# A conditioned decoder trunk on one core: another list of the order of issue

## The chip, the cores and the metric

One core of a Trainium2 chip runs the kernel. The metric is device time in microseconds (us) of one execution, as a median of several. The engines of the core work side by side, each through its own row of instructions in order: TensorE (PE, with its weight loads as PEld), VectorE (DVE), ScalarE (ACT), GpSimd (POOL) and SyncE (SP), which here issues the transfers (DMA) of the weights. An instruction that waits holds up all that stand behind it on its engine. So the same instructions in another order can take another time.

## The reference

Two layers of a decoder trunk on one sequence of 256 tokens of 1024 features (fp32). Each layer normalises x, scales and shifts it by vectors that are made from the conditioning vector c (adaLN: c times `w_ada`), projects it, runs attention, multiplies by a SiLU gate path, projects back, multiplies by the adaLN gate and adds the result to x. A last RMS norm ends it.

```python
def masked_softmax(s, mask, sink=None):
    s = jnp.where(mask, s, -jnp.inf)
    m = jnp.max(s, axis=-1, keepdims=True)
    ...
    return e / jnp.where(den > 0, den, 1.0)

# layer 0: heads "A": sliding window 128 with sinks (8 heads, 1 key head)
#          heads "B": compressed + selected + window branches, gated (8 heads, 2 key heads)
# layer 1: 16 heads, blocks of 256 keys, which with 256 tokens is plain causal attention
```

The weights that have to be read make up most of the 70.29 MB that the profile shows as read.

## The kernel before

**How products are made.** All products of weights are in a split form: a weight tile of 1 MB is loaded into one of five buffers `raw_101` to `raw_105`, ACT casts it to a high half (`whi`), and DVE subtracts that from the original for a low half (`wlo`). The activations have such halves too (`hhi`, `hlo` of the normalised x; `ghi`, `glo` of the attention's output). Three matmuls (`mm3`) then stand for each product: high by high, high by low, low by high. They add up in the PSUM banks `ps_pj`.

**The opening.** The weights `w_in_even` and the adaLN weights come in pieces, and the first projections run on them row block by row block (`start_ada`, `start_row`, `start_sums`, `start_prep`, `start_mm`). The adaLN vector of a block is added up on DVE (`acc`) or PE, transposed into `ps_m`, and made into scale and shift (`shs`). DVE and ACT then use `shs` to make the block's `oT`, `hhi` and `hlo`.

**adaLN later.** For the second layer and for the gates `ada_wide` loads four tiles of `w_ada` to a vector into the same five buffers. DVE multiplies and adds two rows of each to the accumulator (`acc<-raw,cz,acc`, 1024 wide), and the buffer is free after the second of them.

**Attention.** Scores land in `ps_s` (or in `ps_pj`, `ps_m`). DVE masks them and takes the minimum (`late,mn<-ps_s,tb`, printed as ISA or CUSTOM_DVE with a tiny row `mn` behind it), ACT takes the exponential, DVE scales by `rc`, and PE transposes three pieces into the one bank `ps_pt`, from where ACT copies them. `pcT` holds the same for narrower heads, `oT` receives the heads' output, `t` the outputs of projections before they are transposed.

**Parts of the array.** `ada_shift_scale`, `start_sums`, `attn_four`, `attn_values`, `attn_quad` and `compress` use matmuls that fill a part of the array (`tile_position`); those of one set are handed to `plan.group`, which gives each of them all that the set depends on.

**What sets the order.** Nothing is issued as the code is walked. Each call is recorded by `Plan.record` with the calls that it depends on, and `issue` then goes through a list of their numbers, `ORDER`. The engines' rows follow from that list. Since all instructions are issued there, all have that one line in the profile, L249.

```python
    def issue(self):
        place = {i: n for n, i in enumerate(ORDER)}
        assert len(place) == len(ORDER) == len(self.ops)
        for i in ORDER:
            assert all(place[d] < place[i] for d in self.ops[i]["deps"])
            self.ops[i]["inst"] = self.ops[i]["fn"]()
```

Buffers are chosen when a call is recorded, so they do not change with the list.

Of the kernel before, what the change touches and what calls it, by code (L numbers as in the profile page):

```python
# [37 lines left out]
0 2 1 4 5 44 9 685 3 10 6 37 88 11 7 38 35 12 87 13 89 14 15 16 86 17 18 85 19 70 90 20 91 21 71 22 92 55 72 23 93 47  # L38
45 24 41 56 25 48 74 57 26 49 94 73 27 28 40 59 58 80 95 42 29 75 50 30 76 104 60 61 62 51 63 77 78 98 65 64 66 67 106
107 108 109 110 111 112 113 114 115 116 52 117 101 79 118 119 120 121 122 123 124 125 126 127 128 129 53 105 130 131  # L40
132 133 134 135 136 137 96 68 97 138 81 145 139 82 31 69 140 83 32 141 100 33 142 147 34 146 99 182 170 149 164 148
183 151 171 143 150 173 84 179 167 102 165 144 158 185 152 186 176 153 103 177 159 178 156 172 154 174 212 200 201 157
213 160 180 184 155 168 162 206 222 36 187 224 194 166 531 175 225 169 195 181 215 188 226 203 189 207 223 202 227 214
228 229 230 231 232 233 234 235 236 161 237 238 239 240 241 242 243 220 244 245 163 246 247 190 248 197 191 198 208
249 204 217 192 257 196 250 209 251 216 259 252 205 199 258 210 274 261 211 253 286 260 283 255 275 295 254 289 530
268 287 262 193 256 277 219 276 290 218 264 296 292 272 288 221 270 284 273 280 269 281 322 266 293 285 334 263 294
324 282 271 278 291 323 297 335 279 307 313 319 267 325 308 314 310 332 301 265 302 336 316 326 304 303 333 337 338
339 340 341 342 343 344 345 346 347 348 349 329 350 351 352 353 354 355 356 357 305 358 320 309 306 311 327 365 312
359 298 367 317 366 328 299 315 330 360 318 361 321 368 362 300 433 363 371 384 369 436 390 402 364 385 393 370 403
405 529 378 391 437 399 396 373 386 331 372 397 374 394 435 380 379 398 420 387 382 438 432 400 376 401 406 404 381  # L50
423 434 388 407 439 389 421 534 408 392 383 411 440 528 395 429 409 687 414 375 424 441 425 430 377 442 443 444 445
446 447 448 449 450 451 452 453 417 454 415 426 455 418 412 413 456 463 422 457 532 459 410 458 416 533 431 464 427
465 682 480 467 419 466 461 492 489 501 460 478 495 481 469 483 468 486 470 476 484 479 502 683 462 482 474 485 428
490 684 471 491 496 475 507 472 497 513 8 504 477 503 505 506 473 493 498 540 499 541 514 932 555 508 509 686 525 557
487 556 519 809 515 537 526 527 558 538 488 500 543 535 494 510 539 607 520 551 516 511 608 542 553 559 517 552 521
536 518 512 554 545 522 549 560 550 546 565 609 566 544 561 934 562 563 617 564 610 571 931 567 572 568 569 690 616
936 573 629 619 620 621 933 611 622 523 570 630 623 577 612 578 574 575 576 618 524 579 583 580 613 581 688 584 585
586 582 638 589 590 631 624 614 632 637 633 625 591 592 626 634 671 627 587 593 689 588 628 595 596 597 598 635 599
600 640 547 641 636 639 642 643 594 548 601 602 644 603 658 604 605 606 659 650 645 646 664 647 651 648 665 652 653
649 654 660 692 655 691 693 694 661 657 662 695 696 656 697 698 663 699 700 666 810 701 702 935 703 670 704 667 668  # L60
705 672 706 707 669 708 938 709 1014 812 710 811 673 674 956 937 742 39 743 43 744 46 745 675 746 813 747 748 749 940
941 942 943 944 945 946 947 957 1021 756 959 960 961 962 963 964 965 966 939 1024 750 948 949 950 951 754 952 953 954
955 751 676 755 958 677 757 967 968 969 970 971 972 973 974 752 1131 678 753 1209 776 679 975 711 54 774 680 1212 712
778 713 714 758 780 715 782 976 759 977 775 978 760 761 979 681 762 716 768 980 864 865 866 779 867 981 868 615 982
874 869 870 781 871 983 872 777 990 984 985 878 986 987 717 783 896 718 880 719 989 764 763 784 720 902 721 722 723
875 988 724 876 725 991 785 1022 769 992 726 787 727 728 993 729 898 765 766 730 900 731 732 786 767 733 734 994 735
1023 1025 736 995 737 738 739 770 771 772 901 996 792 1330 1026 773 1079 1080 1081 740 1082 1083 1084 903 1085 1086
741 873 788 1091 789 793 790 997 814 815 816 791 817 818 1089 897 998 999 1000 1001 1132 1027 819 820 821 822 823 824
1002 825 1109 826 879 827 1133 1003 794 828 829 877 830 831 832 881 1004 795 796 882 833 1111 834 835 836 1005 837 838
839 1115 840 841 842 1093 843 1116 844 845 1087 846 883 847 899 1113 848 849 1006 850 851 885 852 1210 853 854 855 797  # L70
856 857 858 904 859 1090 860 861 1028 1134 905 1135 862 1136 1137 1138 891 1139 1140 906 1141 884 1215 1337 1007 863
798 799 1338 800 907 801 1211 802 909 803 804 1110 805 886 1114 887 888 890 1029 1030 1088 1008 1031 1032 1033 1142
889 1034 914 1035 1036 1331 915 1037 1038 892 893 1143 894 1039 1040 1041 895 1042 1043 908 1044 1009 1045 1332 1046
1047 1112 1048 1049 910 911 1094 1050 1051 1052 1053 1146 1054 1092 1055 1415 1117 912 1010 1056 1057 1058 806 913
1059 1060 1061 1213 1062 1333 1011 1095 1164 1012 1063 1216 1064 916 917 918 1065 1066 1067 1013 919 1068 1096 1334
1069 1070 807 1071 1072 1073 1074 1015 1075 1165 1335 1148 1098 1214 1016 1149 1076 1017 1018 1104 1019 1166 920 921
1020 1414 922 1144 923 1077 924 1168 1411 925 1170 926 1147 927 1410 1118 1078 1267 1145 1268 1269 1270 1097 1120 1339
1099 1126 1100 1101 1217 1218 1150 1171 1219 928 1220 1221 1222 1102 1223 1224 1151 1340 1225 1226 1167 1227 1228 1229
1230 1169 1231 1232 1233 1153 1234 1103 1235 1236 1416 808 1237 929 1238 1239 1240 1407 1241 1172 1105 1275 1242 1436
1243 1125 1406 1244 1245 1152 1246 1279 1247 1248 1119 1249 1250 1173 1158 1434 1106 1107 1437 1251 1252 1253 1254  # L80
1255 1256 1257 1108 1258 1259 1260 1281 1438 1261 1262 1263 1435 1264 1121 1122 1123 1265 1271 1272 1273 1274 1124
1266 1494 1159 1127 1128 1297 1417 1129 1181 1442 1299 1443 1130 1444 1301 1445 1277 1440 1154 1303 1155 1156 1180
1341 930 1342 1157 1343 1344 1175 1174 1441 1160 1161 1278 1162 1446 1447 1163 1454 1455 1280 1439 1176 1177 1298 1178
1456 1457 1179 1458 1459 1351 1276 1182 1504 1355 1183 1300 1184 1408 1345 1185 1346 1347 1348 1302 1186 1304 1187
1371 1188 1375 1189 1282 1353 1190 1373 1191 1192 1193 1349 1374 1194 1305 1283 1195 1306 1196 1284 1197 1409 1356
1198 1199 1352 1200 1201 1202 1286 1203 1285 1204 1431 1307 1292 1205 1412 1287 1314 1430 1288 1289 1448 1449 1354
1450 1350 1451 1206 1452 1308 1453 1460 1357 1290 1291 1461 1358 1413 1534 1462 1293 1294 1295 1463 1464 1296 1465
1535 1491 1566 1207 1542 1309 1490 1310 1311 1466 1313 1543 1377 1312 1544 1545 1359 1360 1418 1315 1316 1317 1467
1546 1318 1472 1567 1372 1336 1361 1362 1366 1363 1419 1319 1376 1320 1321 1378 1322 1323 1536 1324 1325 1379 1326
1365 1505 1380 1327 1208 1328 1495 1364 1420 1421 1422 1423 1329 1382 1381 1367 1432 1368 1424 1369 1547 1473 1370  # L90
1468 1387 1474 1433 1388 1383 1384 1385 1475 1476 1386 1469 1568 1492 1425 1389 1390 1391 1569 1548 1392 1470 1537
1393 1394 1395 1396 1397 1493 1398 1399 1400 1401 1402 1426 1403 1570 1652 1471 1549 1404 1477 1506 1550 1405 1507
1484 1538 1485 1478 1720 1486 1487 1488 1539 1489 1479 1480 1481 1482 1428 1500 1483 1571 1572 1501 1540 1551 1552
1553 1496 1554 1502 1555 1541 1556 1557 1656 1558 1559 1654 1560 1561 1781 1562 1655 1563 1564 1565 1497 1573 1574
1590 1575 1498 1576 1577 1427 1591 1578 1499 1579 1580 1581 1592 1582 1583 1584 1657 1596 1585 1586 1429 1587 1588
# [1272 lines left out]
```

## Time and profile before

| | before |
|---|---|
| median of 3 runs | 298.81 us (298.41, 300.07, 298.81) |
| span of the profiled execution | 296.8 us |
| PE, DVE, ACT busy | 286.9, 252.2, 188.5 us |
| granted TensorE clock, mean | 0.992 |
| read from memory | 70.29 MB |

The page of the profile does not give the profiled execution's own time beside its span; the runs lie between 1.6 and 3.3 us above the span, and the median 2.0. The stages are found by the names in the trace: the opening to 45 us; the rest of layer 0 and its heads to about 155; the second layer's projections and heads to 252; its output projection to 290; and a tail of 6.4 us, in which the last rows are normalised and stored. A row of a timeline has start in us, duration in us, engine, line, operation, `out<-in`, shape and count, and in brackets the idle time ahead and what ended it.

### The profile page before, as it was taken

How to read it: one execution, taken by the hardware profiler on the slowest of the kernel's cores; microseconds unless marked ns; L12 is line 12 of the kernel's file. 1: busy time of each engine (PE TensorE's matmuls, PEld its weight loads, DVE VectorE, ACT ScalarE, POOL GpSimd, SP SyncE). 2: the span in 40 equal slices, each digit the busy share in tenths (PEclk: the TensorE clock that was granted, in tenths of full speed). 3: DMA queues.
4: the chain of work that ended last, by engine and by line, in shares of the span. 5: the costliest groups of instructions: out<-in, count | busy, mean ns of one | idle time of the engine just before them, and what ended most of it. 6: DMA issues, size and time to landing. Idle time of an engine off the chain costs nothing.

```text
span 296.8 us, 6205 instructions
## 1 busy us (share of the span) xinstructions
PE 286.9 (97%) x2297; PEld 246.3 (83%) x2297; DVE 252.2 (85%) x630; ACT 188.5 (63%) x479; POOL 9.2 (3%) x32
## 2 busy tenths in 40 slices
PE   8999999999999999999999999999999989999991
PEld 8778778897788978776768899998899989887891
DVE  0488698799999999999798679799959779999883
ACT  5356246876997899984638863286386338684531
POOL 2100000001000000000020000000000000000021
PEclk9999999999999999999999999999999999999996
DMA  7999999998992679686886969729828800192003
GB/s 242 389 389 377 344 394 372 300 355 240 390 386 71 235 252 352 210 281 212 305 264 190 367 179 301 275 79 311 300 93 280 280 9 2 42 380 75 3 0 141
DMA packets 48479, 71.73 MB, mean 242 GB/s; under 512 B 2522, under 2 KB 33986, under 8 KB 48450
## 3 DMA queue, kind: packets, MB, share of 16 engines
q1 hardware_dynamic: 47906, 70.92, 70.0%
q10 hardware_dynamic: 544, 0.43, 0.4%
q8 instruction: 18, 0.29, 0.4%
q14 instruction: 11, 0.09, 0.1%
HBM read 70.29 MB, written 1.05 MB: 240 GB/s over the span
## 4 chain that ended last, share of the span: by engine, by line
PE 77%; DMA 14%; DVE 4%; ACT 2%; issue 1%; SPq 1%; POOL 1%; DVEq 0%; ACTq 0%
PE ps_pj L249 53%; PE ps_pt L249 7%; PE ps_o L249 6%; PE ps_s L249 6%; PE ps_m L249 5%; DMA raw<-in_w_in_even_dram 5%; DMA qT<-in_w_ada_dram 4%; DMA raw<-in_w_ada_dram 3%; DMA late<-in_w_ada_dram 2%; DVE wlo L249 1%; ACT whi L249 1%; SPq L249 1%; DVE xs L249 1%; DVE t L249 1%; POOL parts L249 1%
## 5 line engine op out<-in xcount | busy, mean ns | idle before, releaser
L249 ACT CAST whi<-raw 128x512 fp32r<-128x512 f32 (+2 forms) x116 | 72.2, 656 | 23.6 <-PE ps_pj L249 18.5
L249 DVE TENSOR_TENSOR wlo<-raw,whi 128x512 fp32r<-128x512 f32 (+2 forms) x100 | 71.8, 741 | 8.9 <-ACT whi L249 8.8
L249 PE MATMUL ps_pj<-hlo,whi 128*128 128x256 f32 x256 | 69.8, 286 | 0.0
L249 PE MATMUL ps_pj<-hhi,wlo 128*128 128x256 f32 x256 | 69.6, 284 | 0.0
L249 PE MATMUL ps_pj<-hhi,whi 128*128 128x256 f32 x256 | 69.5, 286 | 0.0
L249 PEld LDWEIGHTS ps_pj<-hhi,wlo 128*128 128x128 f32 x256 | 47.4, 188 | 1.7 <-issue 1.3
L249 PEld LDWEIGHTS ps_pj<-hhi,whi 128*128 128x128 f32 x256 | 47.0, 188 | 1.1 <-issue 0.3
L249 PEld LDWEIGHTS ps_pj<-hlo,whi 128*128 128x128 f32 x256 | 47.1, 188 | 0.5 <-issue 0.2
L249 DVE SCALAR_TENSOR_TENSOR acc<-raw,cz,acc 128x1024 f32<-128x1024 f32 x24 | 30.7, 1278 | 2.1 <-DMA raw<-in_w_ada_dram 2.0
L249 ACT ACTIVATE late<-late,mn 128x128 f32<-128x128 f32 (+1 forms) x58 | 25.9, 448 | 8.4 <-DVE mn L249 8.4
L249 DVE SCALAR_TENSOR_TENSOR wlo<-raw,whi 128x512 fp32r<-128x512 f32 x32 | 21.4, 686 | 6.3 <-ACT whi L249 6.2
L249 PE MATMUL ps_pj<-whi,hhi 128*128 128x512 f32 (+2 forms) x72 | 25.7, 376 | 0.6 <-ACT hhi L249 0.5
L249 PE MATMUL ps_pj<-whi,hlo 128*128 128x512 f32 (+2 forms) x72 | 26.0, 372 | 0.0
L249 PE MATMUL ps_pj<-wlo,hhi 128*128 128x512 f32 (+2 forms) x72 | 25.6, 367 | 0.0
L249 ACT COPY late<-ps_pt 128x384 f32<-128x384 f32 (+1 forms) x29 | 14.0, 484 | 12.9 <-PE ps_pt L249 12.9
L249 PE MATMUL ps_pj<-whi,ghi 128*128 128x512 f32 (+1 forms) x56 | 20.8, 372 | 0.0
L249 PE MATMUL ps_pj<-wlo,ghi 128*128 128x512 f32 (+1 forms) x56 | 20.5, 366 | 0.0
L249 PE MATMUL ps_pj<-whi,glo 128*128 128x512 f32 (+1 forms) x56 | 20.4, 366 | 0.0
L249 PE MATMUL ps_pt<-ta,late 128*128 128x128 f32 x87 | 16.5, 278 | 0.9 <-DVE late L249 0.9
L249 PEld LDWEIGHTS ps_pj<-whi,hhi 128*128 128x128 f32 x72 | 13.5, 188 | 3.2 <-ACT hhi L249 1.2
L249 ACT ACTIVATE whi<-raw 128x512 fp32r<-128x512 f32 x16 | 10.0, 629 | 9.0 <-PE ps_pj L249 8.7
L249 PEld LDWEIGHTS ps_pj<-whi,hlo 128*128 128x128 f32 x72 | 13.5, 188 | 1.8 <-issue 0.2
(240 smaller groups left out, 589.6 us busy)
## 6 DMA issues: line engine op xcount, KB each, us to landing
raw<-in_w_in_odd_dram SPq DMA_DIRECT2D x16, 1024.0 KB, 5.8
raw<-in_w_ada_dram SPq DMA_DIRECT2D x8, 1024.0 KB, 7.8
raw<-in_w_ada_dram SPq DMA_DIRECT2D x16, 512.0 KB, 6.0
raw<-in_w_in_even_dram SPq DMA_DIRECT2D x5, 1024.0 KB, 9.0
raw<-in_w_in_even_dram SPq DMA_DIRECT2D x7, 652.0 KB, 6.7
late<-in_w_ada_dram SPq DMA_DIRECT2D x16, 256.0 KB, 6.6
raw<-in_w_out_even_dram SPq DMA_DIRECT2D x4, 1024.0 KB, 5.4
raw<-in_w_out_odd_dram SPq DMA_DIRECT2D x4, 1024.0 KB, 9.2
```

The lines of the kernel that those rows point to most:

```text
L249: self.ops.append(dict(key=eng.key, deps=deps, fn=lambda: getattr(real, name)(*args, **kw)))
```

## The change

The list `ORDER` is replaced by another one that holds the same numbers, and nothing else is edited; the new table has four lines less, so L249 becomes L245. By its description, groups on parts of the array stay whole in it and the opening's loads keep their places. Its first lines before and after:

```diff
-0 2 1 4 5 44 9 685 3 10 6 37 88 11 7 38 35 12 87 13 89 14 15 16 86 17 18 85 19 70 90 20 91 21 71 22 92 55 72 23 93 47
...
+5 0 44 4 9 685 2 3 6 10 37 7 1 88 11 40 38 35 87 12 89 13 14 15 16 17 70 18 86 19 85 20 90 71 21 72 91 22 55 23 45 41 39
```

Three places show what moves. The first is DVE's row where the last heads of layer 1 meet the last adaLN vector (at 237 us in the trace of before). `wlo_116` is the low half of a weight tile, `acc_106<-raw_103` the sum over `w_ada`, `late` score tiles. Before:

```order
L249 SCALAR_TENSOR_TENSOR wlo_116<-raw_101,whi_112 128x4x128
L249 SCALAR_TENSOR_TENSOR acc_106<-raw_103,cz,acc_106 128x1024
L249 ISA late,mn_144<-ps_s_93,tb 128x256
L249 ISA mn_144 128x1
L249 SCALAR_TENSOR_TENSOR wlo_114<-raw_105,whi_110 128x4x128
L249 TENSOR_SCALAR late<-late,rc_149 128x256
L249 ISA late,mn_144<-ps_s_92,tb 128x128
L249 ISA mn_144 128x1
L249 TENSOR_SCALAR late<-late,rc_149 128x128
L249 ISA late,mn_144<-ps_s_92,tb 128x256
```

And now, from the same `wlo_116`:

```order
L245 SCALAR_TENSOR_TENSOR wlo_116<-raw_101,whi_112 128x4x128
L245 SCALAR_TENSOR_TENSOR oT<-ps_o_68,oT 128x512
L245 SCALAR_TENSOR_TENSOR wlo_114<-raw_105,whi_110 128x4x128
L245 ISA late,mn_144<-ps_s_93,tb 128x128
L245 ISA mn_144 128x1
L245 ISA late,mn_144<-ps_pj_96,tb 128x128
L245 ISA mn_144 128x1
L245 ISA late,mn_144<-ps_s_93,tb 128x256
L245 ISA mn_144 128x1
L245 ISA late,mn_144<-ps_s_92,tb 128x256
L245 ISA mn_144 128x1
```

with the sum over `w_ada` further down:

```order
L245 TENSOR_SCALAR late<-late,rc_149 128x128
L245 ISA late,mn_144<-ps_pj_96,tb 128x256
L245 ISA mn_144 128x1
L245 SCALAR_TENSOR_TENSOR acc_106<-raw_103,cz,acc_106 128x1024
L245 RECIPROCAL rc_148<-den_146 128x4
L245 SCALAR_TENSOR_TENSOR wlo_117<-raw_101,whi_113 128x4x128
L245 SCALAR_TENSOR_TENSOR acc_106<-raw_103,cz,acc_106 128x1024
```

The first `acc_106<-raw_103` stood right behind `wlo_116`, ahead of the scores; now it stands 22 rows behind it, after most of them. Its second row came 20 rows after the first and now comes 3 after. The load of `raw_103` is the last of its kind on SP there, behind one of `raw_102` and, in the new list, one of `raw_104` (`w_out_odd`), whose buffer is freed by the second `acc` on `raw_104`: on DVE it stood 29 rows ahead of `wlo_116` and now stands 14 rows ahead.

The second place is the opening, at 35 us, on DVE: `shs` is the scale and shift of the block of features in work, `oT` and `hlo` what is made with it, `wlo_114<-raw_105` the low half of weights that have just landed. Before:

```order
L249 SCALAR_TENSOR_TENSOR acc_106<-qT_99,cz,acc_106 128x512 x2
L249 TENSOR_TENSOR wlo_114<-raw_105,whi_110 128x512
L249 TENSOR_TENSOR shs<-ps_m_107,rT 128x2x2
L249 TENSOR_TENSOR shs<-shs,rT 128x2
L249 TENSOR_TENSOR wlo_114<-raw_105,whi_110 128x512
L249 TENSOR_SCALAR oT<-bigA,shs 128x256
L249 TENSOR_SCALAR acc_106<-late,cz 128x512
L249 TENSOR_TENSOR hlo<-oT,hhi 128x256
L249 TENSOR_TENSOR wlo_115<-raw_105,whi_111 128x512
```

Now:

```order
L245 TENSOR_TENSOR hlo<-oT,hhi 128x256
L245 TENSOR_TENSOR shs<-ps_m_107,rT 128x2x2
L245 TENSOR_TENSOR shs<-shs,rT 128x2
L245 TENSOR_SCALAR oT<-bigA,shs 128x256 x2
L245 TENSOR_TENSOR hlo<-oT,hhi 128x256
L245 TENSOR_SCALAR acc_106<-late,cz 128x512
L245 TENSOR_TENSOR wlo_114<-raw_105,whi_110 128x512 x2
L245 TENSOR_TENSOR wlo_115<-raw_105,whi_111 128x512
```

`shs` and both rows of `oT` have moved ahead of `wlo_114`. On ACT the rows of the same place (`asb` is the vector before its transposition, `whi_110<-raw_105` the casts that `wlo_114` needs) were:

```order
L249 COPY asb_108<-ps_m_107 128x128
L249 CAST whi_110<-raw_105 128x512 x2
L249 ACTIVATE hhi<-bigA,shs 128x256
L249 CAST whi_111<-raw_105 128x152
L249 CAST whi_111<-raw_105 128x512
```

and are:

```order
L245 COPY asb_108<-ps_m_107 128x128
L245 ACTIVATE hhi<-bigA,shs 128x256 x2
L245 CAST whi_110<-raw_105 128x512 x2
L245 CAST whi_111<-raw_105 128x512
L245 CAST whi_111<-raw_105 128x152
```

Both rows of `hhi` now stand ahead of the casts of `raw_105`.

The third place is PE in the projections of layer 0, at about 102 us, where the transposes of three pieces of `bigA` stood together:

```order
L249 MATMUL ps_m_107<-acc_106,ones 128x512
L249 MATMUL ps_pj_94<-hlo,whi_112 128x256
L249 MATMUL ps_pj_94<-hhi,wlo_116 128x256
L249 MATMUL ps_pt_85<-ta,bigA 128x128 x3
L249 MATMUL ps_pj_94<-hhi,whi_113 128x256
L249 MATMUL ps_pj_94<-hlo,whi_113 128x256
L249 MATMUL ps_pj_94<-hhi,wlo_117 128x256
L249 MATMUL ps_pj_94<-hhi,whi_113 128x256
```

and where now single ones stand between the products:

```order
L245 MATMUL ps_pt_85<-ta,bigA 128x128
L245 MATMUL ps_pj_94<-hhi,whi_112 128x256
L245 MATMUL ps_pj_94<-hlo,whi_112 128x256
L245 MATMUL ps_pj_94<-hhi,wlo_116 128x256
L245 MATMUL ps_pj_94<-hhi,whi_112 128x256
L245 MATMUL ps_pj_94<-hlo,whi_112 128x256
L245 MATMUL ps_pt_85<-ta,bigA 128x128
L245 MATMUL ps_pj_94<-hhi,wlo_116 128x256
L245 MATMUL ps_pj_94<-hhi,whi_112 128x256
```

Over the whole program PE has 119 runs of transposes where it had 82. The groups on parts of the array are unbroken in both lists: PE goes into such groups 58 times in the old list and 59 times in the new.

On SP the loads stand in the same order to the end of the opening (`raw_103`, 1304 wide). The next ones (in the new list behind a small `w2v`) were:

```order
L249 DMA raw_104<-in_w_in_even_dram 128x8x256
L249 DMA tb<-in_tbl_b_dram 128x1056
L249 DMA raw_105<-in_w_in_even_dram 128x8x256
L249 DMA raw_103<-in_cmp_w_k_dram 128x8x256
L249 DMA gate<-in_b_ada_dram 128x1024
L249 DMA raw_101<-in_w_in_even_dram 128x8x256
```

and are:

```order
L245 DMA raw_104<-in_w_in_even_dram 128x8x256
L245 DMA tb<-in_tbl_b_dram 128x1056
L245 DMA raw_101<-in_w_in_even_dram 128x8x256
L245 DMA gate<-in_b_ada_dram 128x1024
L245 DMA w2k<-in_cmp_w_k_dram 128x2x64
L245 DMA raw_105<-in_w_in_even_dram 128x8x256
```

`raw_101` has gone ahead of `raw_105`, which holds the weights of the first gate path.

236 rows, old and new, of the table ORDER are left out of this document.

## The prediction

> **What bounds the kernel now.** I read the totals and the shares of the chain first, to see which engine sets the end.
>
> ```profile
> span 296.8 us, 6205 instructions
> PE 286.9 (97%) x2297; PEld 246.3 (83%) x2297; DVE 252.2 (85%) x630; ACT 188.5 (63%) x479; POOL 9.2 (3%) x32
> PE 77%; DMA 14%; DVE 4%; ACT 2%; issue 1%; SPq 1%; POOL 1%; DVEq 0%; ACTq 0%
> ```
>
> PE is busy for 97% of the span and carries 77% of the chain. Its instructions are the same in both lists, so their durations cannot go; only PE's waits can. The second view splits the span at the stages; its columns are the stretch, its length, the busy us of PE, PEld, DVE, ACT and POOL, the granted clock, the DMA share and GB/s.
>
> ```profile
> 14.60:45.00 30.40, 29.79 (x223) 24.38 (x225) 25.43 (x54) 14.68 (x32) 0.00 (x0) 1.00 1.05 376
> 45.00:155.00 110.00, 109.60 (x888) 89.34 (x884) 104.29 (x283) 85.78 (x239) 2.95 (x9) 1.00 0.84 283
> 155.00:238.00 83.00, 83.00 (x677) 76.08 (x673) 68.65 (x157) 50.53 (x117) 0.55 (x1) 1.00 0.73 238
> 238.00:252.00 14.00, 13.09 (x124) 12.36 (x120) 12.00 (x39) 8.83 (x25) 0.00 (x0) 1.00 0.01 3
> ```
>
> PE's visible idle time is 0.61 us in the opening, 0.40 in the long middle, nothing in 155 to 238, and 0.91 in the 14 us of the last heads. That is under 2 us in all, and it caps what a list can gain. A little more hides in the spacing: PE overlaps its instructions, so a short wait shows as a start that comes late while the one before is still called busy. I therefore go by starts, which lie 0.12 us apart for a 128x256 matmul in steady work (239.71 to 239.83 and 258.49 to 258.61, under C), and twice that for one of 512.
>
> The sum is made against the profiled span of 296.8 us. The median of the runs, 298.8, lies 2.0 above it, and I carry those 2.0 unchanged.
>
> **Term A, the last heads: -1.3 us.** First the DMA that the chain follows there, then DVE's timeline, then PE's starts (start us, us, engine, instruction).
>
> ```profile
> 230.68 9.33 DMA raw<-in_w_ada_dram
> ```
>
> ```profile
> 237.35 0.68 DVE L249 SCALAR_TENSOR_TENSOR wlo<-raw,whi 128x512 fp32r<-128x512 f32 x1
> 240.03 1.28 DVE L249 SCALAR_TENSOR_TENSOR acc<-raw,cz,acc 128x1024 f32<-128x1024 f32 x1 [2.00 <-DMA raw<-in_w_ada_dram]
> ...
> 242.44 0.28 DVE L249 CUSTOM_DVE_ANT_0 late<-ps_s,tb 128x128 f32<-128x128 f32 x1
> 242.65 0.28 DVE L249 TENSOR_SCALAR late<-late,rc 128x128 f32<-128x128 f32 x1
> 242.85 0.41 DVE L249 CUSTOM_DVE_ANT_0 late<-ps_s,tb 128x256 f32<-128x256 f32 x1
> 243.19 0.42 DVE L249 CUSTOM_DVE_ANT_0 pcT<-ps_m,tb 128x256 f32<-128x256 f32 x1
> ...
> 243.96 0.68 DVE L249 SCALAR_TENSOR_TENSOR wlo<-raw,whi 128x512 fp32r<-128x512 f32 x1
> 244.56 0.68 DVE L249 SCALAR_TENSOR_TENSOR oT<-ps_o,oT 128x512 f32<-128x512 f32 x1
> 245.16 0.28 DVE L249 CUSTOM_DVE_ANT_0 pcT<-ps_m,tb 128x128 f32<-128x128 f32 x1
> ```
>
> ```profile
> 241.93 0.27 PE L249 MATMUL ps_pj<-hlo,whi 128*128 128x256 f32 x1
> 243.08 0.30 PE L249 MATMUL ps_pt<-ta,late 128*128 128x128 f32 x1 [0.88 <-DVE late L249]
> ...
> 250.91 0.28 PE L249 MATMUL ps_pj<-hlo,whi 128*128 128x256 f32 x1
> 251.23 0.38 PE L249 MATMUL ps_pj<-hhi,whi 128*128 128x256 f32 x1
> ```
>
> DVE stands still for 2.00 us before an `acc` whose adaLN weights landed only at 240.0, 9.33 us after their issue. Behind it in DVE's row wait the score tiles and their scalings, so PE finds no transpose ready: 241.93 to 243.08 is 1.15, of which 0.12 is normal, a loss of 1.03. DVE then stays late, and PE loses a further 0.20 at 251.23 (0.32 less 0.12) and 0.11 just behind. That is 1.34 in all.
>
> In the new list 22 DVE rows stand between the `wlo` of 237.35 and that `acc`. By starts, a 512-wide row takes 0.60 (243.96 to 244.56, 244.56 to 245.16), a score row 0.21 (128 wide) or 0.34 (256), a scaling 0.20; the tiny `mn` rows are in those steps. The rows are four of 512 (two `wlo`, an `oT`, a `glo`; 2.40), four scores of 128 (0.84), four of 256 (1.36) and a scaling (0.20): 4.80. The first row ends its step at 237.95, so `acc` comes due at 242.75, 2.7 us behind the landing of before.
>
> The load does not keep its landing, though: its queue on SP now has three loads of 1 MB in a row (another one of `w_out_odd` joins), freed at about the same time. The nearest row is the trio issued at 257:
>
> ```profile
> raw<-in_w_out_odd_dram SPq DMA_DIRECT2D x3, 1024.0 KB, 9.1
> ```
>
> The median of that trio is 9.1 us, so its third lands later. Near 230 the last of two took 9.33; one more megabyte at the 376 GB/s of the opening's row costs 2.8, so 230.68 + 9.33 + 2.8 = 242.8 is my late estimate, just when `acc` is due. Bounds: the whole 1.34 if it lands by then, nothing if it lands 2 us later. I take -1.3, as the work ahead of `acc` covers even that late estimate.
>
> **Term B, the opening: -0.5 us.** Here the rows are of PE, ACT and DVE, in order of time.
>
> ```profile
> 35.36 1.14 ACT L249 CAST whi<-raw 128x512 fp32r<-128x512 f32 x2 [0.83 <-DMA raw<-in_w_in_even_dram]
> 35.41 0.27 PE L249 MATMUL ps_m<-ta,asb 128*128 128x128 f32 x1
> 36.62 0.15 DVE L249 TENSOR_TENSOR shs<-ps_m,rT 128x4 f32<-128x4 f32 x1
> 36.75 0.39 PE L249 MATMUL ps_pj<-whi,hlo 128*128 128x512 f32 x1
> 37.01 0.60 ACT L249 ACTIVATE hhi<-bigA,shs 128x256 fp32r<-128x256 f32 x1 [0.51 <-DVE shs L249]
> 37.66 0.50 PE L249 MATMUL ps_pj<-whi,hhi 128*128 128x512 f32 x1 [0.53 <-ACT hhi L249]
> ```
>
> The transpose that `shs` needs is over at 35.68, but on DVE `shs` stands behind the `wlo` of the weights that landed at 35.3 and were being cast until 36.5; so it runs at 36.62, the `hhi` row at 37.01, and PE waits from 36.75 to 37.66 (0.91, against 0.24 for a step of 512: 0.67). In the new list both `shs` rows and both `oT` rows stand ahead of that `wlo`, and on ACT both `hhi` rows ahead of the two casts. `shs` can then run at 35.7, 0.9 earlier, and the wait goes. What is late next are the casts, pushed behind 1.0 us of `hhi`, and the weights of the next block. So I take -0.5, with 0 and -0.8 as bounds (0.67 and the small wait of 0.10 after it).
>
> **Term C, transposes broken up: +0.3 us.** On PE the new list has 119 separate runs of transposes where the old one has 82. A lone transpose between matmuls, and three in a run:
>
> ```profile
> 239.71 0.28 PE L249 MATMUL ps_pj<-hlo,whi 128*128 128x256 f32 x1
> 239.83 0.27 PE L249 MATMUL ps_pt<-ta,pcT 128*128 128x128 f32 x1
> 239.86 0.37 PE L249 MATMUL ps_pj<-hhi,wlo 128*128 128x256 f32 x1
> 240.07 0.28 PE L249 MATMUL ps_pj<-hhi,whi 128*128 128x256 f32 x1
> ...
> 258.49 0.28 PE L249 MATMUL ps_pj<-hlo,whi 128*128 128x256 f32 x1
> 258.61 0.49 PE L249 MATMUL ps_pt<-ta,pcT 128*128 128x128 f32 x3
> 258.85 0.36 PE L249 MATMUL ps_pj<-hhi,wlo 128*128 128x256 f32 x1
> 259.06 0.28 PE L249 MATMUL ps_pj<-hhi,whi 128*128 128x256 f32 x1
> ```
>
> The lone one costs 240.07 - 239.71 - 2 x 0.12 = 0.12, the three 259.06 - 258.49 - 2 x 0.12 = 0.33, or 0.11 each. Cut into three, a run of three costs 0.03 more, 0.015 for each extra run; 37 extra runs are 0.6 at most. Starts are given to 0.01, so 0 is the lower end, and I take the middle, 0.3. The groups on parts of the array are whole in both lists, and PE enters them 59 times where it did 58.
>
> [...]
>
> **Term D, the middle: -0.4 us.** Between 45 and 155 PE idles 0.40 us, in small waits such as this one for DVE:
>
> ```profile
> 152.93 0.66 PE L249 MATMUL ps_pj<-ta,t 128*128 128x128 f32 x4 [0.17 <-DVE t L249]
> ```
>
> Lone transposes give each piece its own moment, so PE waits less for the last of three. But the middle has DVE busy for 104.29 of 110 us: an exchange of rows there can make a new wait as well. I bound it by -0.9 (the idle and about as much hidden in spacing) and +1.0 (as large a wait as the one of A), and take -0.4.
>
> The tail after 290.4, where PE has nothing to do, has the same rows in both lists: 0. **Sum:** -1.3 - 0.5 + 0.3 - 0.4 = -1.9; 296.8 - 1.9 = 294.9 of span, and 296.9 with the 2.0 around it.
>
> **The rivals.**
>
> *The waits come back elsewhere.* In A the trio's third load lands after 242.75. For 2.0 us of DVE's wait PE lost 1.34, so each microsecond late costs about 0.7; at 1.5 late, 1.0 of the 1.3 is given back, and B may be given back by the casts. Left are -0.3 to -0.6, 298.2 to 298.5, say 298.4. For it: the landing and the due time fall within 0.1 us of each other by my working. Against it: near 240 the DMA share is 0.01, so a load delayed there has the queues to itself.
>
> *Slower: the weights of the first gate path.* After the opening, SP now issues `raw_101`, `gate` and `w2k` ahead of the `raw_105` that before stood third. The load in question and ACT's first cast of it:
>
> ```profile
> raw<-in_w_in_even_dram SPq DMA_DIRECT2D x1, 1024.0 KB, 11.9
> ```
>
> ```profile
> 58.96 1.04 ACT L249 CAST whi<-raw 128x1024 fp32r<-128x1024 f32 x1
> ```
>
> It was issued at 43.26 and landed at 55.2, 3.8 us before ACT came to it. Another megabyte ahead of it and the half of `gate` take 2.8 + 1.4 us at 376 GB/s, so it lands at 59.4, 0.4 past ACT's place of before. PE goes through the first products meanwhile, which I put at 1 us more of room. Past 60.3 each microsecond reaches PE, as ACT and DVE have no slack there to catch up. It undoes the sum at 62.2; at 64 the kernel takes 296.9 + 3.7 = 300.6. For it: the DMA queues are full there (1.05 and 0.84), and the load took 11.9 us with fewer ahead. Against it: my estimate of the landing is 2.8 us short of the point where it decides.
>
> *The change does not do what its words say.* The groups were whole before, and the loads of the opening stand in the same order. If the rest of the exchange is neutral the kernel stays at 298.8.
>
> **How the numbers follow.** A change under 0.5% (1.5 us) can hardly be told from none in a measurement of this kernel; so faster means below 297.3, slower above 300.3. My forecast has 0.50, with a range of its own of 295.6 to 297.9 (A at its full 1.34, B at -0.8, C and D to one side; or half of A). The waits that come back have 0.30, the gate path's weights 0.12, no effect 0.08. Of the forecast about four fifths lie below 297.3, and of the first rival a sixth: 0.45 faster. Slower gets most of the gate path and some of D's positive end, 0.14. The rest, 0.41, is the same. To leave out no more than 2 in 10, the range goes from 295.0 (every term at its good end but C) to 300.2 (most of the gate path's cases).
>
> **What would show it.** Right for A: no wait before that `acc`, or one under 0.5, and PE's starts at about 242 without a gap of 1 us. Right for B: `shs` about 0.9 earlier against PE's place in the opening and no gap of 0.67 in front of a matmul on `hhi`. C: PE's starts around lone transposes 0.12 above normal, and a middle (45 to 238) no longer than before by over 0.4. Right for the slower rival: ACT waiting for a load of `w_in_even` at about 60, PE idle behind it for as long. Wrong at all: a wait of more than 1 us on PE at a place that this text does not name, or a median outside 295.0 to 300.2.

## The result, and the profile after

The changed list takes 297.22 us (median of 6 runs, 296.67 to 297.46) where the list of before took 299.14 (6 runs, 298.41 to 300.07): a ratio of 0.9931, with a 95% interval of 0.9908 to 0.9954. That is 1.9 us or 0.7% faster, the size that was forecast. The profiled span went from 296.8 to 295.3 us; each of these executions lies about 1.7 us above its own span. The totals and the shares of the chain, after:

```profile
span 295.3 us, 6184 instructions
PE 286.1 (97%) x2297; PEld 245.7 (83%) x2297; DVE 252.8 (86%) x630; ACT 189.0 (64%) x479; POOL 8.5 (3%) x32
PE 89%; DMA 6%; DVE 1%; issue 1%; ACT 1%; POOL 0%; ACTq 0%; POOLq 0%; DVEq 0%
```

PE is as busy as before, but the chain now runs over PE for 89% instead of 77%: fewer of its steps hang on a transfer (6%, from 14%) or on DVE (1%, from 4%). The stages (length, busy us of PE, PEld, DVE, ACT, POOL, clock, DMA share, GB/s) show where:

```profile
14.60:45.00 30.40, 29.31 (x235) 24.22 (x236) 25.53 (x53) 14.26 (x32) 0.00 (x0) 1.00 1.04 367
45.00:155.00 110.00, 109.79 (x888) 89.46 (x878) 104.43 (x282) 86.91 (x240) 1.85 (x6) 1.00 0.80 279
155.00:238.00 83.00, 83.00 (x666) 76.24 (x662) 69.19 (x160) 50.74 (x117) 0.67 (x1) 1.00 0.72 239
238.00:252.00 14.00, 14.00 (x138) 13.65 (x131) 13.33 (x37) 9.23 (x26) 0.00 (x0) 1.00 0.55 200
```

PE's idle time in the last heads is gone (0.91 before, 0.00 now), that of the middle is halved (0.40, now 0.21), and that of the opening has *grown* (0.61, now 1.09). The gain at the end is the one that was forecast; the load that the `acc` needs (size, us from issue to landing), DVE's timeline at that place, and PE's:

```profile
raw<-in_w_ada_dram SPq DMA_DIRECT2D x1, 1024.0 KB, 11.1
```

```profile
237.06 0.69 DVE L245 SCALAR_TENSOR_TENSOR wlo<-raw,whi 128x512 fp32r<-128x512 f32 x1
...
242.48 0.42 DVE L245 CUSTOM_DVE_ANT_0 late<-ps_pj,tb 128x256 f32<-128x256 f32 x1
242.82 0.08 DVE L245 DVE_READ_ACCUMULATOR2_ANT mn<- 128x1 f32 x1
242.82 1.28 DVE L245 SCALAR_TENSOR_TENSOR acc<-raw,cz,acc 128x1024 f32<-128x1024 f32 x1
```

```profile
241.66 0.28 PE L245 MATMUL ps_pj<-hlo,whi 128*128 128x256 f32 x1
241.78 0.27 PE L245 MATMUL ps_pt<-ta,late 128*128 128x128 f32 x1
...
243.55 0.28 PE L245 MATMUL ps_pj<-hlo,whi 128*128 128x256 f32 x1
243.66 0.28 PE L245 MATMUL ps_pj<-hhi,wlo 128*128 128x256 f32 x1
```

The `acc` that waited 2.00 us starts at 242.82 behind the rows that used to stand behind it, and has no wait: the load, issued at 230.68, landed at 241.8. The prediction had put the `acc` at 242.75. PE makes its transpose at 241.78, 0.12 us behind the row before it, where it had lost 1.03. The opening is another matter. PE's timeline, and ACT's:

```profile
18.61 0.39 PE L245 MATMUL ps_pj<-whi,hlo 128*128 128x512 f32 x1
20.09 0.39 PE L245 MATMUL ps_pt<-whi,hhi 128*128 128x256 f32 x1 [1.09 <-ACT whi L245]
```

```profile
17.67 1.14 ACT L245 CAST whi<-raw 128x512 fp32r<-128x512 f32 x2 [1.36 <-DMA raw<-in_w_in_even_dram]
18.72 0.60 ACT L245 ACTIVATE hhi<-bigA,shs 128x256 fp32r<-128x256 f32 x1
19.42 0.84 ACT L245 CAST whi<-raw 128x512 fp32r<-128x512 f32 x2
```

At 36.75, where term B had its wait, PE's starts now follow each other without a gap:

```profile
36.70 0.40 PE L245 MATMUL ps_pj<-whi,hlo 128*128 128x512 f32 x1
36.94 0.40 PE L245 MATMUL ps_s<-whi,hlo 128*128 128x512 f32 x1
37.17 0.63 PE L245 MATMUL ps_s<-whi,hhi 128*128 128x512 f32 x2
37.64 0.40 PE L245 MATMUL ps_pj<-whi,hlo 128*128 128x512 f32 x1
```

That wait is gone, but 18 us earlier PE now waits from 18.61 to 20.09 (1.48, 0.24 of it the normal step): first for `raw_102`, then for its casts. No sentence of the prediction named that place.

### The profile page after: what moved, and what is told of

Its sections match the earlier page's. It is cut to its first block, busy times and chain, and to the rows that moved or that the text cites. A ratio compares the mean times of both kernels' runs of the same rounds, so it can differ in the third digit from the quotient of the medians.

```text
span 295.3 us, 6184 instructions
## 1 busy us (share of the span) xinstructions
PE 286.1 (97%) x2297; PEld 245.7 (83%) x2297; DVE 252.8 (86%) x630; ACT 189.0 (64%) x479; POOL 8.5 (3%) x32
## 4 chain that ended last, share of the span: by engine, by line
PE 89%; DMA 6%; DVE 1%; issue 1%; ACT 1%; POOL 0%; ACTq 0%; POOLq 0%; DVEq 0%
PE ps_pj L245 59%; PE ps_s L245 9%; PE ps_pt L245 8%; PE ps_o L245 7%; PE ps_m L245 6%; DMA raw<-in_w_in_even_dram 3%; DMA rows<-in_b_ada_dram 2%; DMA gate<-in_w_ada_dram 2%; DVE t L245 1%; DVE xs L245 1%; POOL parts L245 0%; ACT t L245 0%; ACTq L245 0%; POOLq L1359 0%; ACT whi L245 0%
## 5 line engine op out<-in xcount | busy, mean ns | idle before, releaser
L245 ACT CAST whi<-raw 128x512 fp32r<-128x512 f32 (+2 forms) x116 | 72.2, 657 | 27.7 <-PE ps_pj L245 17.8
L245 DVE TENSOR_TENSOR wlo<-raw,whi 128x512 fp32r<-128x512 f32 (+2 forms) x100 | 72.0, 741 | 7.7 <-ACT whi L245 7.4
L245 PE MATMUL ps_pj<-hhi,whi 128*128 128x256 f32 x256 | 70.2, 291 | 0.0
L245 PE MATMUL ps_pj<-hlo,whi 128*128 128x256 f32 x256 | 69.5, 287 | 0.0
L245 PE MATMUL ps_pj<-hhi,wlo 128*128 128x256 f32 x256 | 69.3, 287 | 0.0
L245 PEld LDWEIGHTS ps_pj<-hhi,whi 128*128 128x128 f32 x256 | 46.8, 188 | 2.1 <-issue 1.1
L245 PEld LDWEIGHTS ps_pj<-hhi,wlo 128*128 128x128 f32 x256 | 46.8, 188 | 1.0 <-issue 0.7
L245 PEld LDWEIGHTS ps_pj<-hlo,whi 128*128 128x128 f32 x256 | 47.1, 189 | 0.3
L245 ACT ACTIVATE late<-late,mn 128x256 f32<-128x256 f32 (+1 forms) x58 | 26.0, 450 | 7.9 <-DVE mn L245 7.7
L245 DVE SCALAR_TENSOR_TENSOR acc<-raw,cz,acc 128x1024 f32<-128x1024 f32 x24 | 30.7, 1279 | 0.1
L245 DVE SCALAR_TENSOR_TENSOR wlo<-raw,whi 128x512 fp32r<-128x512 f32 x32 | 21.4, 686 | 8.4 <-ACT whi L245 8.4
L245 PE MATMUL ps_pj<-wlo,hhi 128*128 128x512 f32 (+2 forms) x72 | 25.5, 377 | 0.0
L245 PE MATMUL ps_pj<-whi,hhi 128*128 128x512 f32 (+2 forms) x72 | 25.3, 373 | 0.0
L245 PE MATMUL ps_pj<-whi,hlo 128*128 128x512 f32 (+2 forms) x72 | 25.1, 375 | 0.0
L245 PE MATMUL ps_pj<-whi,glo 128*128 128x512 f32 (+1 forms) x56 | 20.7, 370 | 0.0
L245 PE MATMUL ps_pj<-wlo,ghi 128*128 128x512 f32 (+1 forms) x56 | 20.6, 372 | 0.0
L245 PE MATMUL ps_pj<-whi,ghi 128*128 128x512 f32 (+1 forms) x56 | 20.6, 371 | 0.0
L245 PE MATMUL ps_pt<-ta,late 128*128 128x128 f32 x87 | 19.9, 274 | 0.0
L245 ACT COPY late<-ps_pt 128x384 f32<-128x384 f32 (+1 forms) x29 | 14.0, 482 | 6.3 <-PE ps_pt L245 6.3
L245 PEld LDWEIGHTS ps_pj<-whi,hhi 128*128 128x128 f32 x72 | 13.4, 188 | 2.6 <-ACT hhi L245 0.6
L245 PEld LDWEIGHTS ps_pj<-whi,hlo 128*128 128x128 f32 x72 | 13.4, 189 | 2.0 <-issue 0.3
L245 PEld LDWEIGHTS ps_pj<-wlo,hhi 128*128 128x128 f32 x72 | 13.2, 188 | 1.9 <-issue 0.2
```

Of the source, the lines that this page charges most:

```text
L245: self.ops.append(dict(key=eng.key, deps=deps, fn=lambda: getattr(real, name)(*args, **kw)))
```

## The experiments

Twelve kernels ran, the changed list itself among them, each beside runs of the list of before on the same chip. Three chips were used, so kernels of different chips are compared by their ratios to those runs, which have 95% intervals.

**Is the new wait in the opening the order's, or the transfer's?** The changed list again, unedited.

> The changed list once more, for the opening. In its first profile the 652-KB load of raw_102 landed at 17.65 us (before: 16.92) though SP issued it 0.3 us earlier, and PE then waited 1.25 us at 18.61. Theory 1 (the order makes that wait): the load lands at 17.6 again and PE waits 1.2 to 1.3 us again. Rival (the transfer's time differs from execution to execution): it lands between 16.6 and 17.2 and the wait is under 0.9 us. Time 297.2, ratio 0.993 by both.

296.97 us, ratio 0.9929 (0.9901 to 0.9957), span 294.4. ACT's and PE's rows of this execution:

```profile
16.95 1.14 ACT L245 CAST whi<-raw 128x512 fp32r<-128x512 f32 x2 [0.58 <-DMA raw<-in_w_in_even_dram]
```

```profile
18.74 0.40 PE L245 MATMUL ps_pj<-whi,hlo 128*128 128x512 f32 x1
19.37 0.39 PE L245 MATMUL ps_pt<-whi,hhi 128*128 128x256 f32 x1 [0.24 <-ACT whi L245]
```

The same program found `raw_102` 0.7 us earlier, and waited 0.4 instead of 1.25. The size of that wait belongs to the execution; only its place is the list's. In the same way PE's visible idle time from 16 to 50 us was 0.62, 0.90 and 1.32 in three profiles of the old opening (before, e_acc_late, e_mid) and 1.09, 0.25 and 1.37 in three of the new (after, after_again, e_open), so the growth seen in the first pair tells nothing of the lists.

**Term A alone.** One number moved in the list of before; then the same number put back in the changed list.

```diff
 (e_acc_late, from before)
-... 2490 2798 2622 2556 ... 2635 2579 2799 2580 ...
+... 2490 2622 2556 ... 2635 2579 2798 2799 2580 ...
 (e_acc_early, from the changed list)
-... 1964 1965 2612 1966 2475 ... 2631 2576 2798 2204 ...
+... 1964 1965 2612 2798 1966 2475 ... 2631 2576 2204 ...
```

> The list of before with one DVE row moved: the first acc over raw_103 goes 20 rows down, right ahead of its second row. Theory (term A): the work ahead of it then lasts to about 242.1, past the landing at 240.0, so DVE does not wait, PE's gaps at 241.93 and 250.9 go, and the span is 1.1 to 1.3 us shorter, 297.6 to 298.0 against 299.1 (ratio 0.9960). Rival (the gain near 240 came from the other moved rows): the gap at 242 stays at 0.7 or more and the time is within 0.3 of before.

> The changed list with that row put back: the first acc over raw_103 right behind wlo_116, where it stood before. The load lands at 241.8 in this list, so by the theory DVE waits from 237.75 to 241.8, about 4.0 us, twice as long as before, and at 0.6 to 0.7 of each microsecond PE loses 2.4 to 2.8: 299.6 to 300.0 (ratio 1.002 to 1.003). Rival (only the scores' own order counts, or the loads): under 1.0 us is lost, 298.2 or less.

e_acc_late: 297.77 us, ratio 0.9958 (0.9936 to 0.9981), as expected: one row alone brings 1.3 us (0.6 to 1.9 by the interval), most of what the whole list brings. Its DVE row, and what is left of PE's wait:

```profile
243.13 2.60 DVE L249 SCALAR_TENSOR_TENSOR acc<-raw,cz,acc 128x1024 f32<-128x1024 f32 x2
```

```profile
249.69 0.28 PE L249 MATMUL ps_pj<-hlo,whi 128*128 128x256 f32 x1
250.31 0.39 PE L249 MATMUL ps_pj<-hhi,whi 128*128 128x256 f32 x1 [0.34 <-DVE t L249]
```

Both `acc` run back to back without a wait, and the gap at 242 is gone; 0.50 remains at 250, which the changed list does not have.

e_acc_early: 304.25 us, ratio 1.0177 (1.0154 to 1.0200). The direction was right and the price far off: 7.0 us above the changed list's 297.22 (7.3 above its 296.97 on this chip) where 2.4 to 2.8 were expected. Its DVE row, PE's rows, and its windows:

```profile
242.30 1.28 DVE L249 SCALAR_TENSOR_TENSOR acc<-raw,cz,acc 128x1024 f32<-128x1024 f32 x1 [4.44 <-DMA raw<-in_w_ada_dram]
```

```profile
241.78 0.28 PE L249 MATMUL ps_pj<-hlo,whi 128*128 128x256 f32 x1
246.94 0.48 PE L249 MATMUL ps_pt<-ta,late 128*128 128x128 f32 x1 [4.88 <-ACT late L249]
...
250.39 0.29 PE L249 MATMUL ps_pj<-hhi,wlo 128*128 128x256 f32 x1
```

```profile
238.00:241.90 3.90, 3.90 (x54) 3.50 (x46) 0.00 (x0) 0.00 (x0) 0.00 (x0) 1.00 0.50 199
241.90:246.90 5.00, 0.16 (x2) 0.00 (x0) 4.60 (x15) 2.51 (x8) 0.00 (x0) 1.00 0.00 0
246.90:250.30 3.40, 3.36 (x16) 3.36 (x17) 3.38 (x12) 1.47 (x5) 0.00 (x0) 0.50 0.39 98
250.30:258.00 7.70, 7.70 (x67) 7.70 (x67) 4.88 (x11) 4.39 (x11) 0.00 (x0) 1.00 0.63 231
```

DVE's wait of 4.44 cost PE 5.04 (241.78 to 246.94, less 0.12), not 0.65 of it, as PE had no work left to cover any (it was busy for 0.16 of those 5.00 us); and behind it PE ran 3.4 us at a granted clock of 0.50: from this transpose to the `hhi,wlo` 16 matmuls on, 3.45 us (246.94 to 250.39) where the changed list takes 1.88 for the same rows (241.78 to 243.66), another 1.6 us. Together 6.6 of the 7.0.

**The opening alone**, and **term B alone.** For the first, the list of before up to the point where PE reaches 48 us (465 numbers) was sorted as in the changed list; for the second, `shs`, `hhi` and one `oT` (360 to 363) were moved ahead of the casts.

```diff
 (e_open)
-before
+sorted(before[:465], key=after.index) + before[465:]
 (e_shs)
-... 327 365 312 359 298 367 317 366 328 299 315 330 360 318 361 321 368 362 300 433 363 371 ...
+... 327 312 359 360 361 362 363 365 298 367 317 366 328 299 315 330 318 321 368 300 433 371 ...
```

> The opening alone: all that the list of before issues until PE reaches 48 us, put in the changed list's order; behind it the list of before. Theory (the shs step gains 0.8 us, the new wait at 18.6 takes 0.7 to 0.9 back): PE stands within 0.3 us of before at 45 us and the time is 298.8 to 299.3 (ratio 0.999 to 1.001). Rival (the new wait is chance): a gain of 0.7 to 1.0, 298.2, ratio 0.997.

> The list of before with term B alone: both rows of shs and the oT row ahead of wlo_114, the hhi row ahead of the casts of raw_105. Theory: PE's wait at 36.75 (0.67 there, 0.53 in another run) goes to under 0.2 and what is gained stays, 0.5 to 0.7 of span, 298.5, ratio 0.998. Rival (the casts, put back by hhi, make PE wait in its place): a wait of 0.4 or more stays between 36 and 38, and the span gains under 0.2.

e_open: 298.58 us, ratio 0.9992 (0.9972 to 1.0011): no difference that can be measured, though the interval (0.8 us faster to 0.3 slower) is wide enough for the forecast 0.5. e_shs: 299.69 us, ratio 1.0027 (1.0015 to 1.0039), slower. Its DVE, ACT and PE rows:

```profile
35.43 0.16 DVE L249 TENSOR_TENSOR shs<-ps_m,rT 128x4 f32<-128x4 f32 x1 [2.21 <-PE ps_m L249]
```

```profile
35.83 0.60 ACT L249 ACTIVATE hhi<-bigA,shs 128x256 fp32r<-128x256 f32 x1 [1.57 <-DVE shs L249]
36.33 1.87 ACT L249 CAST whi<-raw 128x512 fp32r<-128x512 f32 x4
```

```profile
36.47 0.39 PE L249 MATMUL ps_pj<-whi,hlo 128*128 128x512 f32 x1
37.51 0.50 PE L249 MATMUL ps_pj<-whi,hhi 128*128 128x512 f32 x1 [0.65 <-ACT whi L249]
```

`shs` moved 1.2 us forward, where 0.9 was forecast, and PE's wait did not go: 1.04 us from start to start, where it was 0.91 before (0.76 and 1.32 in two more profiles of that opening, e_acc_late and e_mid), as the matmul needs `hhi` and the casts, ACT makes one after the other (0.60 and 1.87 us), and now the casts come last (36.33 instead of 35.36).

**Are the opening's waits the transfers'?** Both lists with 3.1 MB less to load in the opening: of the adaLN weights of blocks 2 to 7 only the scale half is loaded, and used for both halves.

```diff
-            Y.dma_start(w[k], src[:, k, 0:2, P * g : P * (g + n)])
+            h = 2 if g < 2 else 1
+            Y.dma_start(w[k][:, :h], src[:, k, 0:h, P * g : P * (g + n)])
+            if h == 1:
+                w[k] = w[k][:, 0, :].unsqueeze(1).to_broadcast([P, 2, P * n])
```

> The list of before, but of the adaLN weights of the later blocks of the opening only the scale half is loaded and used for both (24 loads of 128 KB instead of 256 KB, 3.1 MB less; instructions and order unchanged; the output is then not the reference's). Theory (PE's waits from 17 to 50 us are set by the arrival of the transfers): the weights of 18.6 and 36.7 land 1.5 to 6 us earlier, the waits there (1.2 to 1.9 us in five profiles of this opening) go, and the time falls by 1.2 to 1.9: 297.1 to 297.8, ratio 0.9935 to 0.996. Rival (the order of rows on DVE and ACT makes them): the wait of 0.5 to 1.1 at 36.7 stays, gain under 0.6.

> The changed list with the same halved loads. Theory: its waits in the opening (0.6 to 1.4 us in five profiles) go as well, and with the room on the queues the small wait at 66.6 too: 295.6 to 296.6, ratio 0.988 to 0.992; the distance to the list of before under the same loads shrinks to what the last heads and the middle give, 1.1 to 1.7. Rival: the opening of the changed list is better for its order, the distance stays at 2.0 or more.

h_before: 297.93 us, ratio 0.9968 (0.9951 to 0.9984). h_after: 296.13 us, ratio 0.9909 (0.9883 to 0.9935). ACT's and PE's rows of h_before, where the rows stand in the order of before:

```profile
34.44 1.14 ACT L249 CAST whi<-raw 128x512 fp32r<-128x512 f32 x2
36.12 0.60 ACT L249 ACTIVATE hhi<-bigA,shs 128x256 fp32r<-128x256 f32 x1 [0.53 <-DVE shs L249]
```

```profile
36.76 0.40 PE L249 MATMUL ps_pj<-whi,hlo 128*128 128x512 f32 x1
37.00 0.40 PE L249 MATMUL ps_pj<-whi,hhi 128*128 128x512 f32 x1
```

With the weights there earlier the casts run at 34.44 and the wait is gone (0.24 from start to start), though `shs` still stands behind `wlo`. The adaLN vector did not come earlier with its smaller loads: ACT copies it (`asb`) at 34.28, before at 34.26. So it was the weights. The wait at 17.5 stayed, as `raw_102` still landed at 17.2, so the gain was 1.0 us and not 1.2 to 1.9. The two lists remain 1.8 us apart under these loads, 0.1 above what was expected; with intervals of 0.5 us for the one and 0.8 for the other this does not tell 1.7 from 2.0, the rival's bound.

**The middle.** Alone on the list of before, and left out of the changed list.

```diff
 (e_mid)
-before
+before[:465] + sorted(before[465:2427], key=after.index) + before[2427:]
 (e_nomid)
+sorted(before[:465], key=after.index) + before[465:2427] + sorted(before[2427:], key=after.index)
```

> The middle alone: what the list of before issues while PE is between 48 and 233 us, in the changed list's order; opening and end as before. Theory (terms C and D, and what the matched instructions of the two traces show: PE's lead grows by 0.5 to 0.9 between 38 and 110 and by nothing from there to 235): 0.4 to 0.9 faster, 298.3 to 298.8, ratio 0.997 to 0.9985. Rival (the lead came from the opening's transfers, and broken-up transposes cost what the small waits gain): within 0.2 of before in span.

> Opening and end in the changed list's order, the middle (48 to 233 us) as before. Theory (the middle adds 0.4 to 0.7 behind the changed opening, as PE's lead grows between 38 and 110 in both profiles of the changed list): 297.4 to 297.9, ratio 0.995 to 0.9965, that is 0.4 to 0.7 above the changed list. Rival (the middle gives nothing; the rest is the last heads and the opening): 296.9 to 297.2, ratio 0.993 to 0.994.

e_nomid: 297.63 us, ratio 0.9971 (0.9950 to 0.9993), within its range. Against the runs of before on its own chip it gains 1.3 us by the medians and 0.9 by the ratio, the changed list 1.9 and 2.1; that makes the middle worth 0.6 to 1.2 us, but the intervals of the two ratios overlap, so the size stays loose. e_mid missed by 4 us: 302.52 us, ratio 1.012 (1.009 to 1.015). The reason is DVE's row and the windows near 242:

```profile
242.78 1.28 DVE L249 SCALAR_TENSOR_TENSOR acc<-raw,cz,acc 128x1024 f32<-128x1024 f32 x1 [4.41 <-DMA raw<-in_w_ada_dram]
```

```profile
242.30:245.70 3.40, 0.23 (x2) 0.03 (x1) 2.92 (x9) 1.12 (x3) 0.00 (x0) 1.00 0.00 0
245.70:249.10 3.40, 3.27 (x16) 3.31 (x17) 3.40 (x13) 2.25 (x10) 0.00 (x0) 0.50 0.00 0
```

The middle's list holds the loads that are issued in a burst at 230, and the list of before behind it holds the early `acc`. A list with that burst needs the late `acc` as well: without it, `acc` waits 4.4 us, here and in e_acc_early. The late `acc` does without the burst (e_acc_late).

**Transposes put together again (term C).** In the changed list the transposes of 38 sets were moved to the last of their set: 70 runs instead of 119.

```diff
-... 1068 916 917 1213 1216 1069 1070 1071 1072 1073 1074 1075 918 1076 ...
+... 1068 1213 1216 1069 1070 1071 1072 1073 1074 1075 916 917 918 1076 ...
```

> The changed list with transposes put together again: 76 transposes of 38 sets go to right ahead of the last of their set, 70 runs in place of 119; nothing else moves. By term C (0 to 0.015 us for each extra run) 0 to 0.7 faster than the changed list, 0.35 in the middle: span 293.9 to 295.3 beside 294.4 and 295.3 of the two runs of that list. Rival (lone transposes cost nothing and let the copies and scales start apart): 0.2 to 0.6 slower, as PE waits again for the last of three.

296.77 us, ratio 0.9936 (0.9920 to 0.9951), span 294.9: the same as the changed list within the intervals, which are 0.5 us and more to each side. Neither the cost of term C nor that of its rival can be seen; a cost of 0.3 is not excluded.

**Two attempts to go below the changed list.** f_open moves `hhi` ahead of the casts of `raw_102` and three matmuls ahead of the late piece; f_both also moves the load of `raw_105` ahead of `raw_101`.

```diff
 (f_open, from the changed list)
-... 150 156 ... 180 153 168 ... 161 209 222 188 197 ... 225 194 200 ... 201 206 214 ...
+... 150 153 156 ... 180 168 ... 161 188 194 206 209 222 197 ... 225 200 ... 201 214 ...
 (f_both, besides)
-... 453 809 431 413 ... 427 470 687 463 ...
+... 453 687 809 431 413 ... 427 470 463 ...
```

> The changed list with two moves in the opening: ACT makes hhi ahead of the casts of raw_102 instead of behind two of them (ACT stands idle there for 1.36 us), and PE runs three 512-wide matmuls on the first casts ahead of the 256-wide one on the late piece of raw_102. If the wait at 18.6 is the load's and hhi's together, 0.7 us of work covers it: the wait falls by 0.4 to 0.8, span 294.0 to 294.6, time 296.3 to 296.7, ratio 0.9905 to 0.992. Rival (PE only waits at the next matmul instead): no change, 297.0.

> f_open with one SP row moved as well: the load of raw_105 for the first gate path ahead of raw_101, gate and w2k. The load lands at 56 to 57 instead of 60.6, ACT's wait of 0.67 before its cast at 60.69 goes and PE's wait of 0.32 at 66.1 falls under 0.1: 0.2 to 0.3 less than f_open, 296.7 (ratio 0.993). Rival (ACT is not what PE waits for there): the 0.3 stays.

f_open: 297.02 us, ratio 0.9942 (0.9927 to 0.9957); f_both: 297.42 us, ratio 0.9948 (0.9926 to 0.9971). Neither is faster than the changed list. In f_open the wait at 18.6 fell under 0.2, and PE lost about 0.2 each at 50.8 and 66.1 (by its starts), the second behind this ACT row:

```profile
60.69 1.05 ACT L249 CAST whi<-raw 128x1024 fp32r<-128x1024 f32 x1 [0.67 <-DMA raw<-in_w_in_even_dram]
```

In f_both ACT no longer waits there, but its opening drew a late `raw_102` once more, and the casts start at 17.68 instead of 16.95:

```profile
17.68 1.14 ACT L249 CAST whi<-raw 128x512 fp32r<-128x512 f32 x2 [0.89 <-DMA raw<-in_w_in_even_dram]
```

In these two profiles PE lost at one transfer what the list saved at another; the times do not tell the three lists apart.

## Why the prediction was right, point by point

**The total** was right in sign and size: 1.9 us forecast, 1.9 measured (interval 1.4 to 2.8), though not every term was. One sign that the prediction had set for being wrong did show: a wait of over 1 us on PE at a place that it does not name, the 1.24 at 18.61; in the second profile of the same program that wait was 0.4. The lower end of its range, 295.0, is not what its terms give either: -1.34, -0.8, +0.3 and -0.9 from 298.8 make 296.1.

**Term A** (-1.3) was right in mechanism, place and size, and it was shown by moving one number each way. The late estimate of the landing (242.8) was 1.0 too late: it was 241.8. That `acc` came within 0.1 of its due time is in part luck: the `wlo` at the head began 0.3 earlier than taken (237.06), and DVE waited 0.22 on the way (before 239.19). The rows between are 21 and not 22, which changes no term of the sum. The price of a wait, "each microsecond late costs about 0.7", held only near the one wait it was taken from: at 4.4 us it was over 1 (5.04 for 4.44 in e_acc_early), and the slow clock (0.50 for 3.4 us) came on top.

**Term B** (-0.5) failed. The step that failed is "`shs` can then run at 35.7, 0.9 earlier, and the wait goes". `shs` did run earlier, but alone (e_shs) that made the kernel 0.3% slower, since the matmul needs the casts too and ACT is one row. The sentence after it, "What is late next are the casts", named the right thing and priced it too low: they take the place of `shs` in full. What sets the wait is when the weights land, shown for the wait at 36.75 by h_before (the casts at 34.44 instead of 35.36, and 0.24 from start to start instead of 0.91). Why it is absent in the profiles of the changed list, where `shs` and the casts stand as in e_shs, was not tried apart. PE's own row differs there: it starts the transposition of `asb` at 34.67, 0.17 after ACT's copy, where it took 0.88 before (35.41). The time lost at 18.6 does not explain it, as the second profile lost only 0.4 there and has no wait at 36 either. So that wait went in the new opening, but not by the forecast step alone. Against it stands the wait at 18.6: the four profiles of the new opening (after, after_again, e_open, e_nomid) have none at 36 and 1.2, 0.4, 0.8 and 0.6 at 18.6; three of the old one (before, e_acc_late, e_mid) lost 0.7, 0.5 and 1.1 at 36.7 and 0.2, 0.7 and 0.6 near 18. The sums, 0.4 to 1.2 against 0.9 to 1.6, overlap, and as a whole the opening gives nothing that can be measured (e_open).

**Term C** (+0.3) stays open: joining the runs again gained nothing that can be measured (e_join, 0.9936 against 0.9931), which fits 0, the lower end of its bounds, and does not exclude 0.3.

**Term D** (-0.4) had the right sign: 0.6 to 1.2 with and without the middle, with intervals that overlap. Its reason is not borne out. PE's visible idle time between 45 and 155 did go from 0.40 to 0.21, but it is as low from 50 to 155 in e_open (first row), which has the old middle, and in e_join (second row), where the transposes stand together again, so lone transposes are not what lowered it:

```profile
50.00:155.00 105.00, 104.78 (x849) 85.33 (x851) 100.61 (x271) 81.60 (x231) 2.98 (x9) 1.00 0.82 280
50.00:155.00 105.00, 104.79 (x850) 85.30 (x848) 101.18 (x274) 83.05 (x231) 2.02 (x7) 1.00 0.78 272
```

What the middle gains by stays open.

So the sum rests on A, which was measured, and on smaller parts of which none is known to better than half a microsecond: neither B's gain nor C's cost can be told from none, and D came out at 0.6 to 1.2, loosely and for a reason that is not known. That the total came out at 1.9 is in part luck.

**The rivals.** Of the waits that come back one did, in the opening; at `acc` none did, as the load landed 1.0 us ahead of its need. The load of `raw_105` for the gate path did become late. ACT in the changed list:

```profile
60.94 1.05 ACT L245 CAST whi<-raw 128x1024 fp32r<-128x1024 f32 x1 [0.46 <-DMA raw<-in_w_in_even_dram]
```

ACT waited 0.46 for it (0.67 in f_open), past the 60.3 from which PE was to feel it, and far from the 62.2 from which it decides. The third rival, no effect, fell with the measured time.

## What to carry to other kernels

An instruction that waits for a transfer is to stand as late on its engine as the work behind it allows, above all on an engine that feeds the one that bounds; one such row was worth about 1.3 us here (e_acc_late), and put back early in the changed list it kept DVE waiting for 4.44 us (e_acc_early). Before a row is moved ahead, look at every operand of the matmul that waits, and at what else the engine that makes them has to do: in e_shs the operand that came last was moved ahead, and the other one, made on the same engine, took its place. In this opening, whose DMA share was 1.03 to 1.06 from 16 to 50 us and which gained 1.0 us with 3.1 MB less to load (h_before), no order that was tried gave a gain that could be measured, and one profile of such a stage is not evidence for a difference of half a microsecond (PE's idle time from 16 to 50 us went from 0.25 to 1.37 between two profiles of the new opening); profile the unedited kernel twice.

## What the runs showed of the hardware

Behind two long waits on PE a granted clock of 0.50 was measured. In e_acc_early PE was busy for 0.16 of 5.00 us (241.9 to 246.9), and in the 3.40 us behind that the clock was 0.50, which cost another 1.6 us; the next 7.7 us show 1.00 again. In e_mid it was busy for 0.23 of 3.40 us (242.3 to 245.7), and in the 3.40 us behind that the clock was 0.50 as well. In the list of before, where PE lost 1.03 us at 242, it stayed at 1.00 (238 to 252). What sets the clock was not shown. The slow stretch may not come in each execution: one of the six of e_mid took 300.41 us at a mean clock of 0.993, the other five 302.48 to 303.45 at 0.985 to 0.989. No trace of that one is kept, so how long PE waited in it is not known.

The same 652-KB load, issued at the same place of the list, kept ACT waiting until 17.67 us in one execution of the changed list and until 16.95 in another. Why was not tried.
